# mLSTM query projection and scores: a float32 product against three float32r passes over high and low parts, last 128 columns float32, larger slot rings in list 5

## The chip, the core and the metric

The kernel runs on one core of a Trainium2 chip. A core has five engines that run side by side, each through its own queue in order: TensorE (PE, matrix products into PSUM, with its weight loads as PEld), VectorE (DVE), ScalarE (ACT), GpSimd (POOL) and SyncE (SP, which here issues most of the DMAs). An instruction waits at the head of its queue until the results that it needs are there, and everything behind it waits too. The metric is the device time of one execution in microseconds.

## What is computed

One inference step of a two-layer decoder trunk (native sparse attention, then mLSTM) for a prompt of 512 tokens and 8 sample tokens. All of the reference runs in the kernel; the change touches the mLSTM layer of the prompt, whose part of the reference is, cut down:

```python
D_MODEL, D_INNER, M_HEADS, M_HEAD_DIM, QKV_BLK = 1024, 2048, 4, 512, 4
c = jax.nn.silu(conv)
cb = c.reshape(B, T, nb, QKV_BLK)
q = jnp.einsum('btnj,nji->btni', cb, w_qkv[0]).reshape(B, T, D_INNER)
k = jnp.einsum('btnj,nji->btni', cb, w_qkv[1]).reshape(B, T, D_INNER)
...
S = jnp.einsum('bhtd,bhsd->bhts', qc, kc) * jnp.exp(D - mt[..., None])
num = jnp.einsum('bhts,bhse->bhte', S, vc) + ...
C = carry_decay[..., None, None] * C + jnp.einsum('bhsd,bhs,bhse->bhde', kc, w, vc)
```

The projections of q and k are block diagonal with blocks of 4. The kernel folds them: with `c` (the tile `CT`) as it stands, the scores of a head are `CT.T @ (M.T @ CT)`, where `M` is a block-diagonal 128x128 matrix (`bdm`) that holds the product of the q and k weights.

## The kernel before

All tensors are laid out with features on the 128 partitions and the 512 prompt tokens along the free dimension. The mLSTM width of 2048 is 16 tiles of 128 features, four for each of the four heads; a tile is named by head and place (`hd`, `kt`).

The kernel is written as lists of entries. A function such as `qk` adds entries with `P.op(engine, ..., function)`, and each function issues a few instructions. `P.run(ORDER2, R, NE, MOVEDP2)` then issues the entries of the fifth and longest planned stage, here called list 5, in the order that the tuple `ORDER2` gives. So `ORDER2` is the order of every engine's queue. An entry whose place is in `MOVEDP2` is moved to another engine: a copy on ScalarE goes to VectorE and the other way round, a subtraction, product or sum on VectorE goes to GpSimd and the other way round (`swapped`, line 642). `SLOTS` gives by hand which slot of a ring each tile of a pool takes; a tile that takes a used slot waits for that slot's last readers. The ring `("cella", "row")` has 9 slots of 128x512, `("cella", "bd")` 7 of 128x128.

List 5 holds 933 entries: 191 for TensorE, 282 for VectorE, 225 for ScalarE, 97 for GpSimd and 138 for SyncE once the moves are made. They are:

- `qk` (line 2558), for each of the 16 tiles: `f_bdm` and `f_bdk` build block-diagonal matrices; `f_ctw` weights the tile with a row from DRAM (`wb`); `f_po` is the projection `bdm.T @ CT`, one float32 matmul of 512 columns into PSUM; `f_q` copies it to SBUF; `f_s` adds this tile's part of the head's scores, four float32 matmuls of 512, 384, 256 and 128 columns (the scores are causal) into three PSUM banks; `f_pk`, `f_kwh`, `f_kwl`, `f_c`, `f_cpt` compute the state matrix `C` of the tile (for 13 of the 16 tiles; the other three come after list 5).
- `values` (line 2659), for each head: `f_w`, `f_a`, `f_m` turn the scores into weights, `f_h` and `f_l` split them (`Sh`, `Sl`), `f_n` multiplies them with the split values, `f_sq`, the additions to `acc`, `f_pd`, `f_pq`, `f_x1` to `f_y2` make the norm, `f_u1`, `f_u2`, `f_uh`, `f_ul` the gated and split output.
- `v_split`: the split of the values (`vh`, `vl`).
- `state_step` (line 2233), for 24 of the 32 states of the samples: a load of 2 x 512 KB (`cs`), `run` and `spread` on TensorE, `scale` on ScalarE, `outer` on VectorE, two stores.
- `out_unit` (line 2852): the output projection of the heads before, 12 float32r matmuls of 260 columns for each half (`prod`), with a split of the weights (`whi`, `wlo`) and an addition to `x`.
- `head_open` and `head_close`: small work on the samples; among it the copy into `QZ` that `run` reads.

A product that is not left in float32 is computed in three float32r passes over a high and a low part of each operand, high x high, high x low and low x high. The high part is a copy to float32r, the low part the difference:

```python
def lo_of(out, src, hi, eng=None):
    (eng or V).tensor_sub(out, src, hi.bitcast(F32))

def mm3(out, whi, wlo, xhi, xlo, start, stop):
    PE.matmul(out, whi, xhi, start=start, stop=False)
    PE.matmul(out, whi, xlo, start=False, stop=False)
    PE.matmul(out, wlo, xhi, start=False, stop=stop)
```

After list 5 comes the last list (line 2975): the output projection of head 3, the final norm, the three late tiles of `C`, and the last stores. It needs the split output `uh`, `ul` of head 3 from list 5.

Of the kernel before, what the change touches and what calls it, by code (L numbers as in the profile page):

```python
# [9 lines left out]
F32 = mybir.dt.float32  # L10
F32R = mybir.dt.float32r
# [400 lines left out]
    ("mi", "bd"): (
        0, 1, 2, 3, 0, 0, 1, 3, 0, 3, 2, 3, 1, 2, 1, 0,
    ),
    ("st0", "cse"): (
        0, 1, 2, 2, 1, 0, 1, 2, 0, 1, 2, 0, 1, 2, 0, 1, 0, 2, 1, 2, 0, 2, 1, 0, 1, 0, 2, 0,
    ),
# [2669 lines left out]
```

## Time and profile before

| | us |
|---|---|
| median of 3 runs (lowest to highest) | 995.83 (995.11 to 1001.67) |
| the profiled execution | 999.03 |
| its span, first to last instruction | 996.5 |
| granted clock of TensorE | 1.000 |
| bytes moved by DMA | 197.20 MB |

All instructions have the line number of one helper (L668), since the lists are recorded first and issued later, so groups are told apart by the tiles that they write and read: `mm<-CT,bdm` is `f_po`, `s<-q,CT` is `f_s`, `q<-mm` is `f_q`. A float32 matmul stands in the trace as two records, a float32r pass as one. A record's duration holds the pipeline's latency, so what a matmul costs in a full queue is the distance from its start to the next start. A row of a timeline has the start, the duration, the engine, the operation, `out<-in`, the shapes and a count; the idle time before it and what ended it stand in brackets. A row of grouped instructions has the busy time and the mean of one in ns, then the idle time before them.

### The profile page before, as it was taken

What the parts mean: (1) busy time and instruction counts of PE and PEld (TensorE: products, weight loads), DVE (VectorE), ACT (ScalarE), POOL (GpSimd) and SP (SyncE); (2) the same over time, 40 slices, a digit from 0 to 9 for tenths busy, and PEclk for the clock granted to TensorE, in tenths of its full rate; (3) what the DMA queues carried; (4) which work ended last, traced back from release to release, by engine and by line L of the source; (5) the groups of instructions that cost most, each with busy time, mean ns of one, the idle gap of its engine ahead of it and who ended that gap; (6) DMA issues with size and microseconds to landing.
All of it is one profiled execution on the core that took longest, in us unless ns stands there. A gap on an engine that the chain in (4) does not pass through costs nothing.

```text
span 996.5 us, 22671 instructions
## 1 busy us (share of the span) xinstructions
PE 973.9 (98%) x8329; PEld 860.4 (86%) x8329; DVE 797.8 (80%) x1922; ACT 556.0 (56%) x1224; POOL 336.3 (34%) x404
## 2 busy tenths in 40 slices
PE   7999998999999999999999999999999999999998
PEld 5799998899998878799999997998676768777897
DVE  7988986686499988856777997866787978699986
ACT  6746442423488788633346665547657464854533
POOL 1123434331233345622134224323332345424340
PEclk9999999999999999999999999999999999999999
DMA  8755631333445435644743465987997898987633
GB/s 290 244 165 187 202 117 65 112 112 128 149 123 155 127 109 156 184 155 178 213 159 124 137 215 172 319 283 254 286 313 282 293 323 255 326 281 268 210 128 117
DMA packets 123681, 197.20 MB, mean 198 GB/s; under 512 B 16165, under 2 KB 64550, under 8 KB 123314
## 3 DMA queue, kind: packets, MB, share of 16 engines
q1 hardware_dynamic: 117954, 185.39, 57.1%
q10 hardware_dynamic: 5616, 10.36, 2.8%
q8 instruction: 65, 1.06, 0.4%
q14 instruction: 46, 0.38, 0.1%
HBM read 145.99 MB, written 58.10 MB: 205 GB/s over the span
## 4 chain that ended last, share of the span: by engine, by line
PE 86%; DVE 8%; ACT 2%; DMA 2%; issue 1%; SPq 1%; POOL 0%; ACTq 0%; DVEq 0%; POOLq 0%
PE mm L668 55%; PE s L668 14%; PE t L668 12%; PE d L668 6%; DMA x_t<-in_xT 1%; DVE plo L668 1%; SPq L668 1%; DVE num L668 1%; DVE cs L668 1%; DMA praw<-in_cache 1%; DVE wlo L668 1%; DVE dn L668 0%; DVE x L668 0%; DVE ul L668 0%; ACT zsg L668 0%
## 5 line engine op out<-in xcount | busy, mean ns | idle before, releaser
L668 PE MATMUL mm<-hhi,whi 128*128 128x260 f32 x928 | 266.5, 287 | 0.2 <-DVE whi L668 0.2
L668 PE MATMUL mm<-hhi,wlo 128*128 128x260 f32 x928 | 262.4, 283 | 1.4 <-DVE wlo L668 1.4
L668 PE MATMUL mm<-hlo,whi 128*128 128x260 f32 x928 | 262.0, 282 | 0.0
L668 PEld LDWEIGHTS mm<-hhi,whi 128*128 128x128 f32 x928 | 174.7, 188 | 3.2 <-ACT zsg L668 0.8
L668 PEld LDWEIGHTS mm<-hhi,wlo 128*128 128x128 f32 x928 | 174.7, 188 | 1.9 <-DVE wlo L668 1.8
L668 PEld LDWEIGHTS mm<-hlo,whi 128*128 128x128 f32 x928 | 174.7, 188 | 1.1 <-issue 0.5
L668 POOL TENSOR_TENSOR wlo<-wraw,whi 128x512 fp32r<-128x512 f32 (+1 forms) x34 | 63.2, 1861 | 150.4 <-ACT whi L668 47.2
L668 DVE SCALAR_TENSOR_TENSOR cs<-t,wk,cs 128x512 f32<-128x512 f32 x128 | 88.5, 743 | 16.7 <-ACT cs L668 14.6
L668 DVE TENSOR_TENSOR wlo<-wraw,whi 128x1024 fp32r<-128x1024 f32 (+1 forms) x65 | 74.4, 1145 | 10.7 <-ACT whi L668 6.9
L668 ACT ACTIVATE whi<-wraw 128x1024 fp32r<-128x1024 f32 (+1 forms) x60 | 51.8, 868 | 54.7 <-PE mm L668 31.6
L668 ACT ACTIVATE cs<-cs,SBC 128x1024 f32<-128x1024 f32 x64 | 71.2, 1140 | 9.4 <-PE d L668 9.4
L668 ACT ACTIVATE s<-s,mn 128x256 f32<-128x256 f32 (+3 forms) x128 | 70.5, 555 | 7.6 <-DVE mn L668 4.9
L668 POOL TENSOR_SCALAR s<-s,sm 128x256 f32<-128x256 f32 (+3 forms) x53 | 50.6, 965 | 53.5 <-DVE sm L668 26.8
L668 PE MATMUL mm<-uh,whi 128*128 128x260 f32 x224 | 64.9, 290 | 0.7 <-DVE cs L668 0.7
L668 PE MATMUL mm<-uh,wlo 128*128 128x260 f32 x224 | 63.6, 284 | 1.0 <-POOL wlo L668 1.0
L668 PE MATMUL mm<-ul,whi 128*128 128x260 f32 x224 | 63.2, 282 | 0.0
L668 DVE CUSTOM_DVE_ANT_0 s<-s,D 128x128 f32<-128x128 f32 (+3 forms) x128 | 58.3, 486 | 5.5 <-PE s L668 4.0
L668 PE MATMUL s<-phi,w1a 128*128 128x256 f32 (+1 forms) x224 | 49.1, 297 | 0.0
L668 DVE TENSOR_TENSOR plo<-praw,phi 128x256 fp32r<-128x256 f32 (+1 forms) x50 | 41.3, 836 | 7.6 <-ACT phi L668 3.4
L668 PE MATMUL mm<-uo,whi 128*128 128x260 f32 x256 | 46.2, 283 | 0.0
L668 PEld LDWEIGHTS mm<-uh,whi 128*128 128x128 f32 x224 | 42.1, 188 | 2.4 <-DVE cs L668 0.8
L668 PEld LDWEIGHTS mm<-uh,wlo 128*128 128x128 f32 x224 | 42.1, 188 | 1.7 <-POOL wlo L668 1.4
(506 smaller groups left out, 2569.6 us busy)
## 6 DMA issues: line engine op xcount, KB each, us to landing
cs<-in_state_C SPq DMA_DIRECT2D x64, 512.0 KB, 5.6
o_cs<-cs SPq DMA_DIRECT2D x64, 512.0 KB, 4.4
praw<-in_cache SPq DMA_DIRECT2D x128, 128.0 KB, 3.3
dk<-in_cache SPq DMA_DIRECT2D x128, 128.0 KB, 2.6
wraw<-in_m_in SPq DMA_DIRECT2D x32, 512.0 KB, 4.0
wraw<-in_m_out SPq DMA_DIRECT2D x32, 256.0 KB, 4.7
wraw<-in_w_kv SPq DMA_DIRECT2D x11, 512.0 KB, 5.1
wraw<-in_w_q SPq DMA_DIRECT2D x8, 512.0 KB, 3.3
```

Source lines behind the costliest of these rows:

```text
L668: return f(*[real(x) for x in a], **{n: real(x) for n, x in k.items()})
```

## The change

In `qk`, both float32 products of a tile become float32r passes over split operands:

- the matrix `bdm` is split into `bh` and `bl` (128x128), the tile `CT` into `ch` and `cl` (128x512); `f_po` becomes three passes of 512 columns;
- the projection is read from PSUM three times: `f_qh` copies it to float32r, `f_ql` takes the difference (both 128x512), `f_qf` copies its last 128 columns in float32;
- `f_s` becomes three passes each for the blocks of 512, 384 and 256 columns, and the last block of 128 columns stays one float32 matmul with `qf`.

The rings grow: `row` from 9 slots to 15, `bd` from 7 to 13. Six more entries for each of 16 tiles make 1029 entries; `ORDER2`, `MOVEDP2` and the slot lists of list 5 are new throughout. After the moves there are 191 entries on TensorE, 328 on VectorE, 261 on ScalarE, 111 on GpSimd and 138 on SyncE. List 5's own work is otherwise the same, and nothing outside it is edited.

```diff
+    ROWB, BDB = 15, 13
...
-        bdk, bdm, ctw, q, kwh, kwl, cpt = (Tile_(n) for n in ("bdk", "bdm", "ctw", "q", "kwh", "kwl", "cpt"))
+        bdk, bdm, ctw, kwh, kwl, cpt = (Tile_(n) for n in ("bdk", "bdm", "ctw", "kwh", "kwl", "cpt"))
+        bh, bl, ch, cl, qf, qh, ql = (Tile_(n) for n in ("bh", "bl", "ch", "cl", "qf", "qh", "ql"))
...
+        def f_bh():
+            X["bh"] = c2.tile([128, 128], F32R, name="bh", tag="bd", bufs=BDB)
+            S.activation(X["bh"], X["bdm"], AF.Copy)
+
+        def f_bl():
+            X["bl"] = c2.tile([128, 128], F32R, name="bl", tag="bd", bufs=BDB)
+            lo_of(X["bl"], X["bdm"], X["bh"])
+
+        def f_ch():
+            X["ch"] = c2.tile([128, T], F32R, name="ch", tag="row", bufs=ROWB)
+            S.activation(X["ch"], ct, AF.Copy)
+
+        def f_cl():
+            X["cl"] = c2.tile([128, T], F32R, name="cl", tag="row", bufs=ROWB)
+            lo_of(X["cl"], ct, X["ch"])
...
         def f_po():
             X["po"] = mmb()
-            PE.matmul(X["po"], X["bdm"], ct, start=True, stop=True)
-
-        def f_q():
-            X["q"] = c2.tile([128, T], F32, name="q", tag="row", bufs=9)
-            S.activation(X["q"], X["po"], AF.Copy)
+            mm3(X["po"], X["bh"], X["bl"], X["ch"], X["cl"], True, True)
+
+        def f_qf():
+            X["qf"] = c2.tile([128, 128], F32, name="qf", tag="bd", bufs=BDB)
+            S.activation(X["qf"], X["po"][:, 384:512], AF.Copy)
+
+        def f_qh():
+            X["qh"] = c2.tile([128, T], F32R, name="qh", tag="row", bufs=ROWB)
+            S.activation(X["qh"], X["po"], AF.Copy)
+
+        def f_ql():
+            X["ql"] = c2.tile([128, T], F32R, name="ql", tag="row", bufs=ROWB)
+            lo_of(X["ql"], X["po"], X["qh"])
...
-                PE.matmul(st_out(hd, j), ct[:, ks], X["q"][:, 128 * j:], start=kt == 0 and j < 3, stop=kt == 3,
-                          skip_group_check=True)
+                if j == 3:
+                    PE.matmul(st_out(hd, j), ct[:, ks], X["qf"], start=False, stop=kt == 3, skip_group_check=True)
+                    continue
+                for n, (a, b) in enumerate((("ch", "qh"), ("ch", "ql"), ("cl", "qh"))):
+                    PE.matmul(st_out(hd, j), X[a][:, ks], X[b][:, 128 * j:], start=kt == 0 and n == 0,
+                              stop=kt == 3 and n == 2, skip_group_check=True)
...
+        P.op("ACT", 0.2, due - 4, f_bh, r=[bdm], new=[bh])
+        P.op("DVE", 0.2, due - 3, f_bl, r=[bdm, bh], new=[bl], lock=True)
+        P.op("ACT", 0.6, due - 3, f_ch, r=[CTI[ft]], new=[ch])
+        P.op("DVE", 0.68, due - 2, f_cl, r=[CTI[ft], ch], new=[cl], lock=True)
+        P.op("PE", 0.95, due, f_po, r=[bh, bl, ch, cl], new=[po])
+        P.op("ACT", 0.2, due + 1, f_qf, r=[po], new=[qf])
+        P.op("ACT", 0.6, due + 1, f_qh, r=[po], new=[qh])
+        P.op("DVE", 0.68, due + 1.6, f_ql, r=[po, qh], new=[ql])
```

(The figures in `P.op` are notes of a planner that made the order; they are not read when the kernel is built.)

More of the change, by code (lines that the diff above doesn't have):

```diff
@@ L415 @@
     ("st0", "cse"): (
-        0, 1, 2, 2, 1, 0, 1, 2, 0, 1, 2, 0, 1, 2, 0, 1, 0, 2, 1, 2, 0, 2, 1, 0, 1, 0, 2, 0,
+        0, 1, 2, 2, 1, 0, 1, 2, 0, 1, 2, 0, 1, 0, 2, 1, 0, 2, 1, 2, 0, 2, 1, 0, 2, 1, 0, 2,
     ),
@@ L427 @@
     ("st", "cs"): (
-        0, 1, 2, 3, 0, 1, 2, 3, 2, 1, 0, 3, 0, 1, 2, 3, 1, 3, 0, 1, 2, 1, 0, 3, 0, 1, 2, 3, 0, 1, 2, 3, 0, 3, 1, 2,
+        0, 1, 2, 3, 0, 1, 2, 3, 2, 1, 0, 3, 1, 0, 2, 3, 0, 2, 3, 1, 0, 3, 1, 2, 0, 3, 2, 1, 0, 2, 3, 1, 2, 0, 3, 1,
     ),
@@ L435 @@
     ),
+    ("cella", "row"): (
[4 rows of a table added]
+    ),
     ("cella", "bd"): (
-        0, 1, 2, 3, 4, 5, 6, 0, 1, 3, 2, 4, 6, 3, 1, 2, 1, 5, 5, 5, 0, 4, 5, 6, 1, 2, 3, 5, 4, 0, 1, 6,
-    ),
-    ("cella", "row"): (
-        0, 1, 2, 3, 4, 5, 6, 7, 8, 3, 2, 1, 4, 7, 0, 3, 2, 1, 4, 5, 2, 3, 5, 4, 2, 3, 5, 4, 7, 3, 2, 4, 7, 1, 8, 3,
-        0, 1, 5, 2, 4, 5, 1, 7, 0, 3, 8, 1, 2, 7, 1, 4, 5, 0, 2, 4, 7, 3, 1, 5, 2, 6, 2, 4, 1, 7, 3, 4, 6, 5, 1, 3,
[3 rows of a table added]
+    ),
+    ("fw", "w"): (
+        0, 1, 2, 3, 4, 5, 1, 0, 2, 3, 4, 1, 0, 5, 2, 4, 3, 1, 0, 2, 5, 4, 3, 0, 1, 3, 2, 5, 1, 0, 4, 5, 1, 2, 3, 1,
+        0, 4, 5, 2, 1, 0, 3, 2, 5, 4, 0, 3, 1, 2, 4, 5, 3, 0, 1, 4, 2, 5, 0, 3, 1, 2, 5, 4, 0, 1, 3, 4, 5, 2, 0, 3,
+        1, 2, 4, 5, 3, 0,
     ),
     ("cellb", "row"): (
-        0, 1, 2, 3, 4, 5, 2, 0, 1, 3, 4, 1, 0, 2, 5, 0, 3, 2, 1, 4, 5, 3, 2, 1, 0, 5, 4, 3, 2, 1, 4, 3, 1, 5, 0, 3,
-        1, 2, 4, 5,
-    ),
-    ("fw", "w"): (
-        0, 1, 2, 3, 4, 5, 1, 0, 3, 1, 5, 4, 2, 0, 1, 3, 2, 4, 5, 0, 3, 2, 1, 5, 0, 2, 3, 4, 2, 5, 0, 1, 4, 0, 3, 4,
-        0, 5, 2, 3, 1, 4, 3, 2, 0, 5, 4, 3, 0, 5, 1, 2, 3, 4, 0, 2, 4, 3, 0, 5, 1, 3, 2, 4, 0, 2, 4, 1, 5, 3, 0, 4,
-        2, 5, 3, 1, 0, 4,
+        0, 1, 2, 3, 4, 5, 3, 0, 2, 1, 5, 4, 0, 3, 2, 0, 4, 3, 1, 5, 3, 4, 1, 2, 3, 5, 0, 4, 1, 2, 0, 4, 1, 5, 3, 0,
+        4, 1, 2, 5,
     ),
@@ L2566, in rows @@
             def rows():
-                D["wb_", hd] = c2.tile([128, T], F32, name="wb", tag="row", bufs=9)
+                D["wb_", hd] = c2.tile([128, T], F32, name="wb", tag="row", bufs=ROWB)
                 SP.dma_start(D["wb_", hd], rd[hd, 1].unsqueeze(0).to_broadcast([128, T]))
@@ L2579, in f_bdk @@
         def f_bdk():
-            X["bdk"] = block_diag(c2, wc[:, 1, ft], "bdk", 7, "bd")
+            X["bdk"] = block_diag(c2, wc[:, 1, ft], "bdk", BDB, "bd")
         def f_bdm():
-            X["bdm"] = block_diag(c2, mw[:, ft], "bdm", 7, "bd")
+            X["bdm"] = block_diag(c2, mw[:, ft], "bdm", BDB, "bd")
+        def f_bh():
[10 more added lines that the diff above has]
+            lo_of(X["cl"], ct, X["ch"])
         def f_ctw():
-            X["ctw"] = big("ctw", n=T) if late else c2.tile([128, T], F32, name="ctw", tag="row", bufs=9)
+            X["ctw"] = big("ctw", n=T) if late else c2.tile([128, T], F32, name="ctw", tag="row", bufs=ROWB)
             V.tensor_tensor_reduce(X["ctw"], ct, D["wb_", hd], 1.0, 0.0, op0=OP.mult, op1=OP.add,
@@ L2604, in f_kwh @@
         def f_kwh():
-            X["kwh"] = c2.tile([128, T], F32R, name="kwh", tag="row", bufs=9)
+            X["kwh"] = c2.tile([128, T], F32R, name="kwh", tag="row", bufs=ROWB)
             S.activation(X["kwh"], X["pk"], AF.Copy)
         def f_kwl():
-            X["kwl"] = c2.tile([128, T], F32R, name="kwl", tag="row", bufs=9)
+            X["kwl"] = c2.tile([128, T], F32R, name="kwl", tag="row", bufs=ROWB)
             lo_of(X["kwl"], X["pk"], X["kwh"])
@@ L2626, in f_cpt @@
         def f_cpt():
-            X["cpt"] = c2.tile([128, T], F32, name="cpt", tag="row", bufs=9)
+            X["cpt"] = c2.tile([128, T], F32, name="cpt", tag="row", bufs=ROWB)
             S.activation(X["cpt"], X["pc"], AF.Copy)
@@ L2631, in qk @@
         P.op("DVE", 0.77, due - 1, f_ctw, r=[CTI[ft], D["wb", hd]], w=[("cwn", hd, kt)], new=[ctw], lock=True)
-        P.op("PE", 0.95, due, f_po, r=[bdm, CTI[ft]], new=[po])
-        P.op("ACT", 0.6, due + 1, f_q, r=[po], new=[q])
+        P.op("ACT", 0.2, due - 4, f_bh, r=[bdm], new=[bh])
[6 more added lines that the diff above has]
+        P.op("DVE", 0.68, due + 1.6, f_ql, r=[po, qh], new=[ql])
         if not late:
@@ L2638, in qk @@
         st = D["st", hd]
-        P.op("PE", 2.25, due + 2, f_s, r=[CTI[ft], q], w=["st%d" % hd] + ([] if kt == 0 else st), new=st if kt == 0 else [])
+        P.op("PE", 2.25, due + 2, f_s, r=[CTI[ft], qf, qh, ql, ch, cl], w=["st%d" % hd] + ([] if kt == 0 else st), new=st if kt == 0 else [])
         if not late:
@@ L2900, in step_kernel @@
             held += [D["pn", hd], D["wk", hd], D["pr", hd]]
-    P = Plan({**CAPS, "bdk": 5, "bdm": 2, "ctw": 2, "q": 2, "kwh": 1, "kwl": 1, "cpt": 2, "wb": 1, "zs": 1, "ab": 1, "wt": 2,
+    P = Plan({**CAPS, "bdk": 5, "bdm": 2, "ctw": 2, "qf": 2, "qh": 2, "ql": 2, "ch": 2, "cl": 2, "bh": 2, "bl": 2, "kwh": 1, "kwl": 1, "cpt": 2, "wb": 1, "zs": 1, "ab": 1, "wt": 2,
               "Sh": 1, "Sl": 1, "acc": 1, "sq1": 1, "hx": 1, "hy": 1, "fraw": FWB[0], "fhi": FWB[1], "flo": FWB[2]},
```

126 rows, old and new, of tables (MOVEDP2, ORDER2, SLOTS) are left out of this document.

## The prediction

> **What bounds the kernel now.** I read the page first (its busy shares and the chain that ended last), then a table of stretches over the part that list 5 orders, then the waits of VectorE, then single rows for prices.
>
> ```profile
> PE 973.9 (98%) x8329; PEld 860.4 (86%) x8329; DVE 797.8 (80%) x1922; ACT 556.0 (56%) x1224; POOL 336.3 (34%) x404
> PE 86%; DVE 8%; ACT 2%; DMA 2%; issue 1%; SPq 1%; POOL 0%; ACTq 0%; DVEq 0%; POOLq 0%
> ```
>
> ```profile
> core 0: us, PE busy (x) PEld busy (x) DVE busy (x) ACT busy (x) POOL busy (x), PEclk, DMA share, GB/s
> 711.00:740.00 29.00, 28.55 (x172) 17.60 (x173) 28.05 (x67) 17.88 (x26) 11.20 (x18) 1.00 0.89 292
> 740.00:813.00 73.00, 73.00 (x425) 52.82 (x424) 57.02 (x116) 43.16 (x72) 25.33 (x27) 1.00 0.87 300
> 813.00:880.00 67.00, 65.66 (x541) 53.70 (x541) 52.41 (x114) 38.77 (x66) 31.83 (x29) 1.00 0.89 292
> 880.00:960.00 80.00, 78.78 (x636) 66.97 (x635) 76.14 (x159) 38.30 (x69) 25.29 (x27) 1.00 0.75 251
> 711.00:960.00 249.00, 245.99 (x1768) 191.09 (x1769) 213.62 (x453) 138.11 (x232) 93.66 (x100) 1.00 0.84 281
> ```
>
> The first row pair says that TensorE carries the end (86% of the chain). The table says that this is not the whole story inside list 5, which runs from about 711 to 960 us. TensorE is busy in 246.0 of 249 us. VectorE is busy in 213.6 and idle in 35.4, and its idle time is spread unevenly: 16.0 us in 740 to 813, 14.6 in 813 to 880, but 1.0 in 711 to 740 and 3.9 in 880 to 960. In those last 80 us both engines are full. ScalarE (138) and GpSimd (94) have room everywhere, and the clock is 1.00 throughout.
>
> ```profile
> DVE cs L668 <- ACT cs L668: 9.9, 7, 4.3
> DVE hx L668 <- ACT hx L668: 4.1, 2, 3.3
> DVE x L668 <- PE mm L668: 3.5, 4, 1.6
> DVE dn L668 <- PE t L668: 3.1, 1, 3.1
> ```
>
> These are VectorE's longest waits (total, times, longest). They are waits in a fixed queue for results that TensorE or ScalarE gave late. They are slack as long as TensorE is the bound; the question is how much of it new VectorE work can fill.
>
> **TensorE: what the passes save.** Prices are start to start, since matmuls overlap.
>
> ```profile
> 728.35 2.77 PE mm L668 x12
> 765.24 0.89 PE t L668 x8
> 766.13 0.86 PE mm L668 x2
> 766.99 2.16 PE s L668 x8
> 919.08 0.39 PE L668 MATMUL mm<-Sh,vh 128*128 128x512 f32 x1
> ...
> 920.67 0.22 PE L668 MATMUL mm<-Sh,vh 128*128 128x128 f32 x1
> ...
> 920.95 0.45 PE L668 MATMUL mm<-Sh,vh 128*128 128x512 f32 x1
> ```
>
> Here 766.13 is one `f_po` (a float32 product of 512 columns, two records): 0.86 us. 766.99 is one `f_s` (512, 384, 256 and 128 columns in float32, eight records): 2.16. 728.35 is one `f_c`, twelve float32r passes of 512 columns: 2.77, or 0.23 each. So the new `f_po` costs 3 x 0.23 = 0.69, a gain of 0.17. From 919.08 to 920.67 run nine float32r passes, three each of 512, 384 and 256 columns, exactly what the new `f_s` issues: 1.59. Its last block stays a float32 product of 128 columns; 765.24 holds four of those in 0.89, so 0.22. (Three passes of 128 took 920.67 to 920.95, 0.28, so leaving that block in float32 is right.) New `f_s`: 1.81, a gain of 0.35. Sixteen tiles: 16 x (0.17 + 0.35) = **8.3 us less TensorE work**. This price is firm: the same shapes and types stand in the trace.
>
> **VectorE: what the splits cost.** I set the new list 5 and its moved entries against the code, entry by entry. The 16 of each new kind run: `f_bl` 5 on VectorE and 11 on GpSimd; `f_cl` 7 and 9; `f_ql` all 16 on VectorE; `f_bh` 10 on VectorE and 6 on ScalarE; `f_ch` 4 and 12; `f_qf` 5 and 11; `f_qh` 2 and 14. The old `f_q` had 5 on VectorE and 11 on ScalarE.
>
> ```profile
> 947.41 1.89 DVE L668 TENSOR_TENSOR num<-num,zs 128x512 f32<-128x512 f32 x3
> 715.15 0.42 DVE L668 CAST vh<-VT 128x512 fp32r<-128x512 f32 x1
> L668 DVE TENSOR_TENSOR bdm<-cst,mw 128x128 f32<-128x128 f32 x6 | 1.7, 280 | 0.0
> L668 DVE COPY q<-mm 128x512 f32<-128x512 f32 x5 | 3.4, 683 | 0.0
> L668 DVE SCALAR_TENSOR_TENSOR wt<-s,wt 128x128 f32<-128x128 f32 x4 | 1.1, 280 | 0.0
> ```
>
> Three 128x512 operations take 1.89 with 0.08 of overlap each: 0.60 a piece. Less the same overlap a 128x512 cast is 0.34, a PSUM copy of 128x512 0.60, a 128x128 operation 0.20. The trace has no 128x128 cast on VectorE; it lies between nothing and the 0.20 above, and I take 0.14. Sum: `f_bl` 1.0, `f_cl` 4.2, `f_ql` 9.6, `f_bh` 1.4, `f_ch` 1.4, `f_qf` 1.0, `f_qh` 1.2, less 3.0 for `f_q`: 16.8 us. The other entries that change engine (five more additions to `acc`, four more `ul` and two more `Sl` come to VectorE, three `vl`, a copy of `ncs`, a `cpt` and some casts go) come to about 2. So **19 us more VectorE work**.
>
> ```profile
> L668 DVE TENSOR_TENSOR kwl<-t,kwh 128x512 fp32r<-128x512 f32 x13 | 8.9, 686 | 2.9 <-ACT kwh L668 2.7
> L668 DVE TENSOR_TENSOR ul<-num,uh 128x512 fp32r<-128x512 f32 x8 | 6.5, 839 | 1.1 <-POOL ul L668 1.1
> 910.01 1.77 DVE L668 TENSOR_TENSOR Sl<-wt,Sh 128x512 fp32r<-128x512 f32 x1
> ```
>
> VectorE is also stretched now and then: a subtraction with one PSUM input (`kwl`) takes 686 ns on the mean, the same shape with both inputs in SBUF (`ul`) 839, one `Sl` 1.77 us. The excess is 0.15 for `ul`; about 14 more such operations on VectorE and more GpSimd work beside them make about 2 us. Total: 21, so VectorE busy goes from 213.6 to **234.6 us**. [...]
>
> **The other engines.**
>
> ```profile
> L668 ACT ACTIVATE vh<-VT 128x512 fp32r<-128x512 f32 x10 | 6.2, 619 | 0.7 <-issue 0.7
> L668 ACT ACTIVATE q<-mm 128x512 f32<-128x512 f32 x11 | 6.5, 589 | 3.8 <-PE mm L668 3.8
> L668 ACT ACTIVATE onesr<-ones 128x128 fp32r<-128x128 f32 x1 | 0.3, 299 | 0.0
> L668 POOL TENSOR_TENSOR vl<-VT,vh 128x512 fp32r<-128x512 f32 x8 | 10.7, 1333 | 13.3 <-DVE vl L668 11.3 <-ACT vh L668 1.8
> L668 POOL TENSOR_TENSOR bdm<-cst,mw 128x128 f32<-128x128 f32 x10 | 4.0, 404 | 8.6 <-PE t L668 8.6
> ```
>
> ScalarE gains 12 `f_ch` at 0.62, 6 `f_bh` and 11 `f_qf` at 0.30 and three more copies at 0.59: 14 us, hidden in its 111 idle us. GpSimd gains 11 x 0.40 + 9 x 1.33 = 16 and gives about 8 away: hidden too. SyncE keeps its 138 entries and all bytes; loads stand in another order, DMA is 0.84 busy over the stretch, and the same bytes in 246 us make 0.85. I price that and the larger rings of slots (row 9 to 15, bd 7 to 13, which issue nothing) at nothing; a load or a slot that comes late would show as a VectorE or ScalarE wait, so the ends are those of the idle time below.
>
> The chain for one tile grows: the product now waits for `f_ch` and `f_cl`, and the scores wait for `f_qh` and then `f_ql`. Behind a late `f_ql` stand VectorE's `outer` entries, which stores wait for, and behind a late `f_s` all of TensorE. The tightest place in the new list is tile 3 of head 2, where between `f_po` and `f_s` TensorE has one `f_s` and one `spread` (over 2.0 us), against 0.6 + 0.6 plus hand-over for the chain. It fits. The opening doesn't:
>
> ```profile
> 711.45 1.12 PE mm L668 x2
> 712.58 2.21 PE d L668 x16
> ```
>
> Before, two `f_po` run ahead of or during the wait for `QZ`; now the first `f_po` stands behind the 16 products of 712.58 and needs a cast, two subtractions and `f_bdm` of VectorE after it has written `QZ`. I take 1.5 us lost there (between 0 and the 2.5 that both products and one subtraction take).
>
> **The sum.** If TensorE stayed the bound the part would shorten by 8.3 to 240.7, and VectorE, busy 234.6, could idle in only 6. I don't believe it. Where both engines are full in this trace (880 to 960) VectorE still idles 3.9 of 80, or 4.8%. At that rate 234.6 becomes 246.4: **a gain of 2.6 us**.
>
> A second count agrees. The last stage begins with
>
> ```profile
> 876.58 0.86 PE t L668 x2
> 877.56 0.68 DVE L668 SCALAR_TENSOR_TENSOR hx<-t,hx 128x512 f32<-128x512 f32 x1
> 957.79 1.42 DVE L668 TENSOR_TENSOR x<-x,mm 128x260 f32<-128x260 f32 x4
> ```
>
> which are `f_pq` and `f_x4` of head 2 and the end of list 5 on VectorE: 82 us, VectorE full. Behind that `f_x4` stood 100 VectorE entries and now stand 104, nine of them new (4 us) for others that went. So this stage doesn't shorten. Ahead of that `f_pq` TensorE saves 12 tiles' worth, 6.2 us, but has 133 entries instead of 130 (about 3 us at 1 us each) and loses 1.5 at the opening: 2 us left. What TensorE saves in head 3 is late for nobody: VectorE is late next. I take **2.3 us less**. The profiled execution took 999.03 (2.5 around its span of 996.5), so such a one would take 996.7; the median of the runs is 995.83, 3.2 lower, so I say **993.5**.
>
> **The rivals.** *VectorE keeps its idle time* (the other side). For it: its waits above are for ScalarE's `cs` and `hx`, not for TensorE alone, and a fixed queue with two more hand-overs per tile fills badly. Against: the first and the last stage fill it. Price: with 25 of 35.4 us kept, 234.6 + 25 = 259.6, 10.6 more than 249, so 1006.4. It turns into a loss where more than 14.4 us of idle stay.
>
> *TensorE stays the bound.* For it: 246 of 249 busy, new entries placed early (34 of the 49 new VectorE entries stand ahead of `f_x4` of head 1, where 17 us were idle). Against: the 6 us that it leaves VectorE. Price: 8.3 less, 987.5; with the 3 us that TensorE now idles saved as well, 984.5.
>
> *GpSimd and VectorE block each other in full.* For it: 910.01. Against: the mean excess is 0.15 of 1.3. If each of the net 8 us of new GpSimd work held VectorE up, VectorE would be 8 us later: 246.4 + 8 - 2 (counted already) = 252.4, 3.4 slower, 999.2. [...]
>
> **Chances.** My forecast, with TensorE and VectorE both near full and -6 to +3 us: 0.58. TensorE stays the bound: 0.17. Blocking in full: 0.10. VectorE keeps its idle time: 0.15. A measurement of this kernel can tell about 1% (10 us) from no change. Faster by more than that needs the second rival with its stalls gone: 0.10. Slower by more than that needs most of the first: 0.13. The rest, 0.77, is within 1%. The range of 985 to 1004 runs from the TensorE bound with part of its stalls gone to 22 us of VectorE idle (+7.6, 1003.4).
>
> **What would show it.** In the after profile `f_po` should take 0.7 and `f_s` 1.8 start to start, and TensorE's busy time from 711 to the end of list 5 should be under 240. VectorE's busy time there should be near 234 with 8 to 16 idle. If VectorE's idle is over 20, with TensorE waits on `ql` or `cl`, the first rival holds; if TensorE is full and VectorE waits for it, the second; if `wlo`, `ul` and `cl` rows of VectorE exceed 1 us often, the third. A price of a float32r pass far from 0.23 would make the whole sum wrong.

## The result and the profile after

| | before | after |
|---|---|---|
| median of 20 runs each, side by side on one chip (lowest to highest) | 997.66 (995.11 to 1002.52) | 990.37 (987.80 to 996.94) |
| the profiled execution | 999.03 | 989.0 |
| its span | 996.5 | 987.3 |

The changed kernel takes 0.9933 of the time before, with a 95% interval of 0.9918 to 0.9949: 6.7 us less (5.1 to 8.2). The median of 995.83 us, from which the prediction started, was that of the first three runs; over twenty it is 997.66.

All instructions now have line L677. The page's busy shares and the chain that ended last, of the kernel after:

```profile
PE 966.8 (98%) x8393; PEld 868.4 (88%) x8393; DVE 810.3 (82%) x1968; ACT 568.2 (58%) x1260; POOL 342.3 (35%) x418
PE 7%; DVE 4%; issue 1%; ACT 1%; POOL 0%; DVEq 0%; ACTq 0%; POOLq 0%
```

TensorE has 64 more records and is busy 7.1 us less. The chain could be followed back over the last eighth of this execution only, so its shares can't be set against the 86% of before. Its pieces can be read (start, duration, what):

```profile
875.67 0.68 DVE hx L677
...
888.56 1.81 PE s L677 x11
...
922.06 1.41 DVE cs L677 x2
...
946.75 1.79 DVE ul L677 x3
```

A new `f_s` takes 1.81 us, as worked out. From 922 to 949 us the chain goes no longer through TensorE but, bar a few pieces, through VectorE: the norm of head 3 and what stands in its queue. (875.67 is `f_x4` of head 2.)

The same table of stretches as before, cut at 953 us, just behind the new end of list 5 (950.3):

```profile
core 0: us, PE busy (x) PEld busy (x) DVE busy (x) ACT busy (x) POOL busy (x), PEclk, DMA share, GB/s
711.00:740.00 29.00, 29.00 (x199) 22.77 (x193) 25.09 (x63) 23.11 (x41) 15.01 (x24) 0.98 0.90 301
740.00:813.00 73.00, 72.96 (x493) 59.74 (x492) 68.17 (x144) 50.85 (x92) 35.18 (x40) 1.00 0.90 307
813.00:880.00 67.00, 64.51 (x535) 54.04 (x534) 63.39 (x125) 35.49 (x60) 23.91 (x24) 1.00 0.89 298
880.00:953.00 73.00, 72.56 (x615) 63.79 (x614) 70.07 (x162) 39.37 (x72) 27.08 (x29) 1.00 0.74 247
711.00:953.00 242.00, 239.03 (x1835) 200.34 (x1829) 226.72 (x490) 148.81 (x265) 101.18 (x116) 1.00 0.85 286
```

VectorE is busy in 226.7 of 242 us, where it was busy in 213.6 of 249. In the two middle stretches (740 to 880) its idle time has gone from 30.6 us to 8.4. TensorE is still full (239.0 of 242 us). VectorE's waits:

```profile
DVE cs L677 <- ACT cs L677: 5.7, 6, 2.2
DVE ql L677 <- ACT qh L677: 1.7, 2, 1.3
```

The waits for `hx`, `mm` and `dn` of before are gone or short; 5.7 us for ScalarE's `cs` remain, and 1.7 us for the new `qh`.

Prices of the new VectorE work, first by groups, then two rows of the opening, and the end of list 5 on VectorE:

```profile
L677 DVE TENSOR_TENSOR ql<-mm,qh 128x512 fp32r<-128x512 f32 x16 | 10.9, 685 | 1.9 <-ACT qh L677 1.7
L677 DVE TENSOR_TENSOR cl<-CT,ch 128x512 fp32r<-128x512 f32 x7 | 6.4, 922 | 0.0
```

```profile
708.66 0.23 DVE L677 CAST bh<-bdm 128x128 fp32r<-128x128 f32 x1
708.80 1.29 DVE L677 TENSOR_TENSOR cl<-CT,ch 128x512 fp32r<-128x512 f32 x2
...
946.66 1.97 DVE L677 TENSOR_TENSOR ul<-HN,uh 128x8 fp32r<-128x8 f32 x4
948.55 1.75 DVE L677 TENSOR_TENSOR x<-x,mm 128x260 f32<-128x260 f32 x5
```

`f_ql` takes what a subtraction with a PSUM input took before (`kwl`, 686 ns). Two `f_cl` take 1.29 us where nothing is beside them, 0.65 each, but 922 ns on the mean: two of the seven last longer, 1.23 us at 778.37 and 1.81 at 868.50, the one beside GpSimd's `Sl` (778.21, 0.84 us) and `bl` (779.02, 0.91), the other beside its `vl` (868.47, 1.29).

TensorE's own waits in list 5:

```profile
PE d L677 <- DVE QZ L677: 2.0, 1, 2.0
PE mm L677 <- DVE kwl L677: 1.8, 1, 1.8
...
PE mm L677 <- DVE ql L677: 0.2, 1, 0.2
```

The two long waits stand at single places; for a new split (`ql`) it waits 0.2 us in all.

Not all of the 9.2 us between the two spans belongs to the change. The row `t<-pr,ones`, the same piece of work just ahead of list 5 in both kernels, starts at 708.06 us before and 705.10 after (both rows are shown below). So 3.0 us had been gained where the two kernels are the same, and 6.2 us from there on, which agrees with the runs.

### The profile page after: what moved, and what is told of

Read it like the earlier page. It is cut to its first block, busy times and chain, and to the rows that moved or that the text cites. A ratio compares the mean times of both kernels' runs of the same rounds, so it can differ in the third digit from the quotient of the medians.

```text
span 987.3 us, 22906 instructions
## 1 busy us (share of the span) xinstructions
PE 966.8 (98%) x8393; PEld 868.4 (88%) x8393; DVE 810.3 (82%) x1968; ACT 568.2 (58%) x1260; POOL 342.3 (35%) x418
## 5 line engine op out<-in xcount | busy, mean ns | idle before, releaser
L677 PE MATMUL mm<-hhi,whi 128*128 128x260 f32 x928 | 266.4, 287 | 0.2 <-DVE whi L677 0.2
L677 PE MATMUL mm<-hhi,wlo 128*128 128x260 f32 x928 | 262.4, 283 | 1.4 <-DVE wlo L677 1.3
L677 PE MATMUL mm<-hlo,whi 128*128 128x260 f32 x928 | 262.0, 282 | 0.0
L677 PEld LDWEIGHTS mm<-hhi,whi 128*128 128x128 f32 x928 | 174.7, 188 | 3.2 <-PE d L677 0.8
L677 PEld LDWEIGHTS mm<-hhi,wlo 128*128 128x128 f32 x928 | 174.8, 188 | 2.1 <-DVE wlo L677 2.0
L677 PEld LDWEIGHTS mm<-hlo,whi 128*128 128x128 f32 x928 | 174.7, 188 | 1.1 <-issue 0.5
L677 POOL TENSOR_TENSOR wlo<-wraw,whi 128x512 fp32r<-128x512 f32 (+1 forms) x35 | 64.4, 1842 | 121.9 <-DVE whi L677 43.1
L677 DVE SCALAR_TENSOR_TENSOR cs<-t,wk,cs 128x512 f32<-128x512 f32 x128 | 88.7, 742 | 11.2 <-ACT cs L677 10.4
L677 DVE TENSOR_TENSOR wlo<-wraw,whi 128x1024 fp32r<-128x1024 f32 (+1 forms) x64 | 73.9, 1155 | 10.4 <-ACT whi L677 6.5
L677 ACT ACTIVATE cs<-cs,SBC 128x1024 f32<-128x1024 f32 x64 | 71.3, 1146 | 12.5 <-PE d L677 10.4
L677 ACT ACTIVATE s<-s,mn 128x256 f32<-128x256 f32 (+3 forms) x128 | 70.6, 555 | 7.6 <-DVE mn L677 4.9
L677 ACT ACTIVATE whi<-wraw 128x1024 fp32r<-128x1024 f32 (+1 forms) x59 | 51.2, 871 | 41.1 <-PE mm L677 26.7
L677 POOL TENSOR_SCALAR s<-s,sm 128x256 f32<-128x256 f32 (+3 forms) x53 | 50.6, 965 | 53.9 <-DVE sm L677 27.1
L677 PE MATMUL mm<-uh,whi 128*128 128x260 f32 x224 | 65.0, 290 | 1.8 <-DVE kwl L677 1.8
L677 PE MATMUL mm<-uh,wlo 128*128 128x260 f32 x224 | 63.6, 284 | 0.3 <-POOL wlo L677 0.3
L677 PE MATMUL mm<-ul,whi 128*128 128x260 f32 x224 | 63.3, 283 | 0.3 <-DVE ul L677 0.3
L677 DVE CUSTOM_DVE_ANT_0 s<-s,D 128x128 f32<-128x128 f32 (+3 forms) x128 | 58.3, 485 | 5.5 <-PE s L677 4.1
L677 PE MATMUL s<-phi,w1a 128*128 128x256 f32 (+1 forms) x224 | 49.1, 297 | 0.0
L677 PE MATMUL mm<-uo,whi 128*128 128x260 f32 x256 | 46.2, 283 | 0.0
L677 PEld LDWEIGHTS mm<-uh,whi 128*128 128x128 f32 x224 | 42.1, 188 | 3.8 <-DVE kwl L677 2.0
L677 DVE TENSOR_TENSOR plo<-praw,phi 128x256 fp32r<-128x256 f32 (+1 forms) x50 | 39.1, 792 | 7.1 <-ACT phi L677 4.0
L677 PEld LDWEIGHTS mm<-ul,whi 128*128 128x128 f32 x224 | 42.2, 188 | 1.3 <-issue 0.5
```

What stands on the lines that cost most here:

```text
L677: return f(*[real(x) for x in a], **{n: real(x) for n, x in k.items()})
```

## The experiments

Each row is a ratio to runs of the kernel before on the same chip. The last column is the difference of its ratio to 0.9933, times 997 us; two such intervals together leave 2.0 to 2.5 us of doubt in it, and more in two runs with few executions: 3.1 in early_unlocked, 3.8 in no_ql_two_passes. Where a length of list 5 is given, it is that of one profiled execution.

| run | median | ratio, 95% interval | against the changed kernel |
|---|---|---|---|
| float32_again | 998.22 | 1.0011 (0.9995 to 1.0028) | +7.8 |
| old_work_new_order | 996.48 | 0.9991 (0.9976 to 1.0006) | +5.8 |
| no_ql | 990.01 | 0.9924 (0.9911 to 0.9937) | -0.9 |
| two_passes | 988.09 | 0.9915 (0.9898 to 0.9933) | -1.8 |
| no_ql_two_passes | 985.33 | 0.9886 (0.9852 to 0.9921) | -4.7 |
| splits_on_vector | 998.25 | 1.0017 (0.9999 to 1.0035) | +8.4 |
| splits_heads01 | 994.58 | 0.9969 (0.9949 to 0.9989) | +3.6 |
| splits_heads23 | 994.50 | 0.9966 (0.9948 to 0.9984) | +3.3 |
| before_unlocked | 997.36 | 0.9999 (0.9984 to 1.0014) | (edit of the kernel before) |
| early_po | 990.02 | 0.9932 (0.9912 to 0.9951) | -0.1 |
| unlocked_alone | 988.27 | 0.9922 (0.9904 to 0.9939) | -1.1 |
| early_unlocked | 987.81 | 0.9897 (0.9871 to 0.9924) | -3.6 |

**float32_again: the products alone undone.** The theory was that TensorE set the time and its saving is the gain; the rival, that the gain came with the new order, the moves and the rings.

```diff
-            mm3(X["po"], X["bh"], X["bl"], X["ch"], X["cl"], True, True)
+            PE.matmul(X["po"], X["bl"].bitcast(F32), X["cl"].bitcast(F32), start=True, stop=True)
...
-                for n, (a, b) in enumerate((("ch", "qh"), ("ch", "ql"), ("cl", "qh"))):
-                    PE.matmul(st_out(hd, j), X[a][:, ks], X[b][:, 128 * j:], start=kt == 0 and n == 0,
-                              stop=kt == 3 and n == 2, skip_group_check=True)
+                PE.matmul(st_out(hd, j), X["cl"].bitcast(F32)[:, ks], X["ql"].bitcast(F32)[:, 128 * j:], start=kt == 0,
+                          stop=kt == 3, skip_group_check=True)
```

> The changed kernel with one float32 matmul again for each projection and for each block of the scores (on the low parts alone, so the products of the high parts are left out); every split and every wait of the change stays. TensorE gets its 8.3 us back, VectorE's work is the same. If TensorE still sets the time of list 5: 6 to 8 us above the changed kernel's 990.4, so 996 to 999. If VectorE sets it, or if the gain is the new order's alone: 0 to 2 above, 990 to 993.

998.22 us, 7.8 us more: all of the gain hangs on the 8.3 us of TensorE work. The profile shows where it falls. These are `f_x4` of head 2 and the end of list 5 on VectorE:

```profile
881.44 0.69 DVE L677 SCALAR_TENSOR_TENSOR hx<-t,hx 128x512 f32<-128x512 f32 x1
956.30 1.75 DVE L677 TENSOR_TENSOR x<-x,mm 128x260 f32<-128x260 f32 x5
```

From the row `t<-pr,ones` to this `f_x4`, and from there to the end, list 5 takes:

| us | to `f_x4` of head 2 | from there to the end |
|---|---|---|
| before | 169.5 | 81.7 |
| float32_again | 176.0 | 76.6 |
| the changed kernel | 170.6 | 74.6 |

The new list, with its splits, shortens the last part by 5.0 us and lengthens the part ahead by 6.5. The passes then take 5.4 and 2.0 us off the two parts, near the 6.2 and 2.1 at which the twelve tiles ahead and the four behind were priced.

**old_work_new_order: the order alone.** The old products and the old copy, without the splits (`f_bh` stays, as a float32 copy), in the new order, with the new moves and rings.

```diff
-            mm3(X["po"], X["bh"], X["bl"], X["ch"], X["cl"], True, True)
+            PE.matmul(X["po"], X["bh"], ct, start=True, stop=True)
...
-            lo_of(X["cl"], ct, X["ch"])
+            R.flip = None
...
-            lo_of(X["ql"], X["po"], X["qh"])
+            R.flip = None
```

> The new order, new moves and larger rings with the old float32 products: no low parts, no f_ch, no f_qf; only f_bh stays, as a float32 copy of the matrix. VectorE has about 15 us less work than in the changed kernel, TensorE 8.3 more. If the gain is the order's (and its fewer collisions): 985 to 991. If TensorE's saving is needed: 996 to 999. If both engines share the bound: in between, 991 to 995.

996.48 us, a ratio of 0.9991 to before: the order, the moves and the rings bring nothing by themselves. The other half, the new work in an order like the old one, wasn't tried, so what the order and the larger rings are worth to the new work stays open.

**no_ql: VectorE lighter.**

```diff
-            lo_of(X["ql"], X["po"], X["qh"])
+            R.flip = None
...
-                for n, (a, b) in enumerate((("ch", "qh"), ("ch", "ql"), ("cl", "qh"))):
+                for n, (a, b) in enumerate((("ch", "qh"), ("ch", "qh"), ("cl", "qh"))):
```

> The changed kernel without the 16 low parts of the projection (f_ql); the second pass of the scores reads the high part once more, so the low part's share is left out and TensorE does the same work. VectorE has 16 x 0.60 = 9.6 us less and the chain from projection to scores is shorter. If VectorE sets the time: 5 to 9 us below 990.4, 981 to 985. If TensorE sets it: 0 to 2 below, 988 to 990.

990.01 us. Taking 9.6 us of work from VectorE brings nothing that can be measured (in the profile its busy time over list 5 falls by 7.0 us, from 228.6 to 221.6). With the first run this makes TensorE the bound of the changed kernel as far as `f_ql` reaches. The last one starts at 896.9 us, so of the end of list 5, where the chain runs through VectorE from 922 us on, the run says nothing.

**two_passes: TensorE lighter.**

```diff
-                for n, (a, b) in enumerate((("ch", "qh"), ("ch", "ql"), ("cl", "qh"))):
+                for n, (a, b) in enumerate((("ch", "qh"), ("ch", "ql"))):
...
-                              stop=kt == 3 and n == 2, skip_group_check=True)
+                              stop=kt == 3 and n == 1, skip_group_check=True)
```

> The changed kernel without the third pass (low part of the tile times high part of the projection) in the scores, which is left out of the sum; all splits stay. TensorE has 16 x 0.53 = 8.4 us less, VectorE the same. If TensorE sets the time: 6 to 8 us below 990.4, 982 to 985. If VectorE sets it: 0 to 2 below, 988 to 990. Both engines at their limit: 2 to 4 below.

988.09 us: of another 8.4 us of TensorE work only about 2 come through (list 5 is 3.6 us shorter, 241.7 against 245.2). TensorE now waits 1.9 us in all for `ql`, where it waited 0.2. Another limit stands right behind TensorE, and the remaining runs ask which one.

**no_ql_two_passes: both lighter.** The two diffs above together.

> From the changed kernel, two cuts together: the 16 f_ql are left out (the second score pass reads qh in place of ql; VectorE -9.6 us) and the third score pass is left out (TensorE -8.4 us). Alone the first gave 990.0 and the second 988.1, against 990.4 for the changed kernel. Theory VECTORE IS NEXT: TensorE sets the time of the changed kernel, and with 8.4 us less of it VectorE, busy 226.7 of 242 us, stops the gain after 2.3 us. With VectorE lighter too, most of the 8.4 us arrive: 982 to 985. Rival SOMETHING ELSE IS NEXT (waits of the fixed order, the opening, loads, the last list): 987 to 988.5, no better than the cut in TensorE alone.

985.33 us. The cut in VectorE, worth 0.9 alone, is worth 2.9 once TensorE is lighter, and TensorE's 1.9 us of waits for `ql` go with it. That points to VectorE as the next limit, but does not show it: the doubt in 2.9 is 3.9 us, and list 5 is only 0.8 us shorter than in two_passes (240.9 against 241.7). Nor is 4.7 the whole 8.4: the first theory's range was just missed, and the rival's too. What keeps the other 3.7 us is not settled. Part of it is TensorE's granted clock at the opening (more on that below): 0.63 and 0.52 in the two stretches of 4 us from 708 in this profile, 0.59 and 0.98 in the changed kernel's, which makes an estimate of 1.7 us.

**splits_on_vector, and its two halves: VectorE heavier.** The places of the 20 `f_cl` and `f_bl` leave the list of moved entries, so GpSimd's share of the splits goes back to VectorE.

```diff
-MOVEDP2: 313, 331, 349, 351, 459, 475, 477, 493, 495 (heads 0 and 1)
-MOVEDP2: 583, 585, 601, 619, 621, 637, 794, 814, 824, 826, 838 (heads 2 and 3)
```

> From the changed kernel, the 9 f_cl and 11 f_bl that run on GpSimd go back to VectorE: VectorE +7.6 us of work by the prices of the prediction, GpSimd -16. Theory VECTORE HAS ROOM (it idles 15 us in list 5): 990 to 992.5. Rival VECTORE IS AT ITS LIMIT: most of 7.6 us comes through, 995 to 998. Third possibility: VectorE is freed of blocks by those 20 GpSimd instructions and gets that much back, so that its busy time rises by less than 7.6.

998.25 us: 8.4 more for 7.6 us of work, so nearly all of it comes through, although VectorE idled 15 us. In the profile VectorE is busy 235.0 us in list 5, against 228.6, so 6.4 of the 7.6 us arrive there; a little is given back, as the third possibility had it. TensorE's waits show how the work comes through:

```profile
PE mm L672 <- DVE cl L672: 2.5, 1, 2.5
PE s L672 <- DVE ql L672: 2.3, 2, 2.1
```

Both are new, bar the 0.2 us for `ql`, and with them list 5 is 4.7 us longer (249.9 against 245.2). This execution, 993.81 us, was the shortest of its twelve. Over the twelve the mean granted clock of TensorE is 0.9948, over the changed kernel's twenty 0.9970; on TensorE's 967 us that makes an estimate of 2 of the 8.4 us. Is it the sum of the work or these two places? Each half was run by itself.

> From the changed kernel, of the 20 f_cl and f_bl that run on GpSimd only the 9 of heads 0 and 1 go back to VectorE (VectorE +3.4 us of work). All 20 together took 998.2 against 990.4. Theory THE AMOUNT: VectorE as a whole is at its limit, so each part brings its own work: 993.5 to 994.5. Rival THE PLACE: the chain of a tile is late where its splits wait their turn in VectorE's queue, and TensorE stands (in the profile of all 20 it waited 2.1 us for a ql of head 1 near 757 us and 2.5 us for a cl): this half brings most of the 7.8 us, 995 to 998, with these TensorE waits in it.

> From the changed kernel, the other 11 of the 20 (heads 2 and 3: 5 f_cl, 6 f_bl; VectorE +4.2 us of work) go back to VectorE. Theory THE AMOUNT: 994 to 995. Rival THE PLACE: 990 to 992, since no TensorE wait of the profile of all 20 stood here but the 2.5 us for a cl.

994.58 and 994.50 us: 3.6 and 3.3 more for 3.4 and 4.2 us of work, about where THE AMOUNT had put them. But each half has kept one of the two waits, heads 0 and 1 first:

```profile
PE s L672 <- DVE ql L672: 2.1, 1, 2.1
```

```profile
PE mm L672 <- DVE cl L672: 2.5, 1, 2.5
```

In the second half's profile list 5 is 3.1 us longer (248.3 us), which is this wait and one of 0.6 us for a `cs`. In the first half's it is 5.0 us longer (250.2): the wait of 2.1, and a lower clock behind it and at the opening (0.994 over this whole execution, against 0.998 in the changed kernel's), each an estimate of 1.7 us from the granted clock of its stretches. So two places, each with its own wait, could give the same medians. The runs don't tell the amount from the places, and the profiles speak for the places.

**before_unlocked: was VectorE the bound of the last stage before?** In the kernel before, six GpSimd entries of the last stage (three `wlo`, three of the gated output of head 2), beside which VectorE's rows stood stretched (from 899 to 927 us rows of 1.59, 1.77, 1.71, 1.22 and 1.30 us, where the shortest of their kinds take 0.68, 0.68, 0.68, 0.19 and 0.17), go to VectorE (one that was moved there leaves the list, one that is written for GpSimd joins it).

```diff
-MOVEDP2: 700, 889
+MOVEDP2: 702, 704, 790, 875
```

> From the kernel before, six GpSimd entries of the last stage (three wlo, three of the gated output of head 2), each of which overlaps a stretched VectorE instruction, are moved to VectorE: VectorE +3.6 us of work, and about 8.7 us of stretch less in that stage. Theory of the prediction (VECTORE SETS THE LAST STAGE of the kernel before): 3 to 5 us faster than before, 992 to 994. Rival TENSORE SETS IT TOO: within 1 us of before, 996.5 to 998, with VectorE's busy time in 880 to 960 lower and its idle time higher.

997.36 us, no change. Some of VectorE's rows in the kernel before, and the same in this one:

```profile
914.22 1.71 DVE L668 TENSOR_TENSOR ul<-num,uh 128x512 fp32r<-128x512 f32 x1
...
917.17 1.22 DVE L668 TENSOR_TENSOR HN<-HN,CS 128x32 f32<-128x32 f32 x1
```

```profile
916.12 0.69 DVE L664 TENSOR_TENSOR ul<-num,uh 128x512 fp32r<-128x512 f32 x1
...
919.16 0.19 DVE L664 TENSOR_TENSOR HN<-HN,CS 128x32 f32<-128x32 f32 x1
```

What took 1.71 and 1.22 us takes 0.69 and 0.19. The stretch of 880 to 960 us in its profile:

```profile
880.00:960.00 80.00, 77.35 (x617) 64.81 (x616) 73.25 (x159) 39.93 (x71) 17.55 (x23) 1.00 0.75 249
```

VectorE's busy time in it is 73.25 us, where it was 76.14. But this execution is the longest of its twelve (1002.21 us) and starts list 5 later (710.40 us against 708.06), so the stretch is not the same work. From `f_x4` of head 2 to the end of the list, in each kernel's own time, VectorE is busy 76.5 of 83.2 us, and was 77.0 of 81.7. It has 2 us more of idle time, and the stage is no shorter. So VectorE did not set the pace of the last stage, and part of its fullness there was stretch, as in the 1.71 and 1.22 us above. That leaves TensorE, busy in 80.4 of those 81.7 us; in the new list float32_again agrees, where 2.1 us less TensorE work there made that part 2.0 us shorter.

**early_po: the opening.** Tiles 0 and 1 of head 0 get one float32 product again, ahead of the first `run`, with `f_bdm` on GpSimd; their `f_bh` and `f_bl` fall away.

```diff
+    EARLY = ((0, 0), (0, 1))
...
         def f_po():
             X["po"] = mmb()
+            if (hd, kt) in EARLY:
+                PE.matmul(X["po"], X["bdm"], ct, start=True, stop=True)
+                return
             mm3(X["po"], X["bh"], X["bl"], X["ch"], X["cl"], True, True)
```

> From the changed kernel, the first two projections (tiles 0 and 1 of head 0) are single float32 products again, as before the change, and stand ahead of the first run; their two f_bdm are on GpSimd, their f_bh and f_bl fall away. TensorE pays 2 x 0.17 = 0.34 us more, VectorE is 0.9 us lighter. Theory THE OPENING COSTS 2 US: TensorE waits 2.03 us for QZ there and the two products (1.7 us) fill the hole, so the scores of tile 0 start 1 to 1.7 us sooner and the time is 988.5 to 989.5. Rival THE HOLE IS HARMLESS: TensorE starts the scores sooner, but the time comes back as a wait further on: 990.0 to 991.0.

990.02 us: nothing that can be measured, with 2.5 us of doubt. The timeline of TensorE at the opening, first of the kernel before, then of the changed one, then of early_po:

```profile
708.06 0.27 PE L668 MATMUL t<-pr,ones 128*32 128x32 f32 x8 [1.33 <-DVE pr L668]
709.71 1.12 PE L668 MATMUL mm<-CT,bdm 128*128 128x512 f32 x2 [0.36 <-POOL bdm L668]
711.45 1.12 PE L668 MATMUL mm<-CT,bdm 128*128 128x512 f32 x2 [0.62 <-DVE bdm L668]
712.51 2.28 PE L668 MATMUL d<-cs,QZ 128*32 128x512 f32 x16
```

```profile
705.10 0.27 PE L677 MATMUL t<-pr,ones 128*32 128x32 f32 x8 [1.33 <-DVE pr L677]
...
708.42 3.53 PE L677 MATMUL d<-cs,QZ 128*32 128x512 f32 x16 [2.03 <-DVE QZ L677]
...
712.79 0.40 PE L677 MATMUL mm<-ch,bh 128*128 128x512 f32 x1
...
713.49 0.62 PE L677 MATMUL t<-VB,OH 128*128 128x512 f32 x2
```

```profile
706.61 0.27 PE L608 MATMUL t<-pr,ones 128*32 128x32 f32 x8 [1.34 <-DVE pr L608]
...
708.25 1.98 PE L608 MATMUL mm<-CT,bdm 128*128 128x512 f32 x4 [0.35 <-POOL bdm L608]
710.17 1.92 PE L608 MATMUL d<-cs,QZ 128*32 128x512 f32 x16
...
714.52 0.39 PE L608 MATMUL s<-qh,ch 128*128 128x512 f32 x1
```

The hole of 2.03 us is filled, and the first scores come 7.9 us after `t<-pr,ones` instead of 9.5 (714.64 in the changed kernel). In the traces list 5 is 1.1 us shorter (from that row to the last `ul`: 242.4 against 243.5 us); in the runs it doesn't show.

**unlocked_alone and early_unlocked: stretched rows in the changed kernel.** Six GpSimd entries of 840 to 872 us (three `f_u2` and an `f_ul` of head 1, two `vl`) go to VectorE, alone and together with the edit before.

```diff
-MOVEDP2: 565, 784, 786
+MOVEDP2: 555, 563, 567
```

> From the changed kernel, two edits together: the first two projections as float32 products ahead of the first run (as in the run early_po), and six GpSimd entries of 840 to 872 us (three products and a subtraction of the gated output of head 1, two vl) on VectorE, where VectorE instructions stood blocked beside them for 6.7 us in sum (one of them, 1.06 us in the norm of the samples, ahead of TensorE's wait of 1.8 us for kwl); VectorE +3.6 us of work. Theory BLOCKS COST HERE: TensorE's 1.8 us wait goes and the opening's 1.1 us that the trace of early_po showed stays saved: 987.5 to 989. Rival VECTORE IS AT ITS LIMIT: the 3.6 us of work undo it: 990 to 993.

> From the changed kernel, only the second edit of early_unlocked: the six GpSimd entries of 840 to 872 us on VectorE, the opening as it is. Both together took 987.8, the opening alone 990.0, the changed kernel 990.4. Theory BLOCKS BRING IT: 988 to 989, with TensorE's wait of 1.8 us for kwl gone and its wait of 2.0 us for QZ still there. Rival BOTH ARE NEEDED: as long as the opening's wait and lowered clock stay, 989.5 to 990.5.

987.81 us for both edits, 3.6 less than the changed kernel (with 3.1 us of doubt) and 0.9897 of the kernel before (0.9871 to 0.9924): the fastest of all kernels here that leave nothing out. The second edit alone has 988.27 us, but by its ratio only 1.1 less, within the doubt. The traces are clearer (VectorE, the changed kernel, then unlocked_alone):

```profile
846.02 1.23 DVE L677 SCALAR_TENSOR_TENSOR hf_v<-rs_t,rs_y 128x8 f32<-128x8 f32 x1
847.28 1.19 DVE L677 TENSOR_TENSOR dn<-hf_v,dn 128x8 f32<-128x8 f32 x1
...
848.62 0.68 DVE L677 TENSOR_TENSOR kwl<-t,kwh 128x512 fp32r<-128x512 f32 x1
```

```profile
846.70 0.17 DVE L672 SCALAR_TENSOR_TENSOR hf_v<-rs_t,rs_y 128x8 f32<-128x8 f32 x1
846.90 0.17 DVE L672 TENSOR_TENSOR dn<-hf_v,dn 128x8 f32<-128x8 f32 x1
...
847.21 0.68 DVE L672 TENSOR_TENSOR kwl<-t,kwh 128x512 fp32r<-128x512 f32 x1
```

And GpSimd and TensorE of the changed kernel at the same time:

```profile
845.92 2.53 POOL L677 TENSOR_TENSOR num<-num,zs 128x512 f32<-128x512 f32 x2
```

```profile
849.36 0.39 PE L677 MATMUL mm<-uh,whi 128*128 128x260 f32 x1 [1.78 <-DVE kwl L677]
```

Two operations on 128x8 that take 0.17 us each took 1.23 and 1.19 beside two GpSimd products; `kwl` behind them came late, and TensorE stood for 1.78 us. In unlocked_alone this wait is gone, and list 5 is 2.7 us shorter (240.8 against 243.5, to the last `ul`). VectorE's busy time over list 5 falls too, from 228.6 to 226.2 us, though it got 3.6 us of work. With the opening's edit added the list is no shorter still (241.0).

## Where the prediction was right and where it failed

The forecast was 993.5 us, within 985 to 1004, with both engines near full; 990.37 came, and both engines are near full. The gain was mis-sized: 2.3 us were forecast and 6.7 came (5.1 to 8.2), just past the 6 that bounded my own case, and nearer to the 8.3 of the rival in which TensorE stays the bound. That the time itself lies only 3.1 us from the forecast is in part luck: the three runs from which I started had a median of 995.83 us and twenty have 997.66, and the errors of the steps below partly cancel. By its steps:

- **TensorE saves 8.3 us: right.** A new `f_po` takes 0.70 us (712.79 to 713.49), a new `f_s` 1.81; 16 x (0.16 + 0.35) = 8.2. Putting the old products back costs 7.8.
- **TensorE as the only bound, 8.3 us less: nearly reached.** 6.7 of the 8.3 us came. TensorE does set the time while VectorE gets lighter (no_ql), but it waits 1.8 us for a late `kwl`, and 2.0 at the opening.
- **Both engines near full: right, and closer than thought.** 8.3 us more TensorE work cost 7.8, and 7.6 us more VectorE work 8.4; 8.4 us less on TensorE brought about 2, and 9.6 less on VectorE about 1, each with some 2 us of doubt. So another limit, most likely VectorE's queue, lies some 2 us behind TensorE's.
- **VectorE's work, 19 us more: right as far as the rows go.** `f_ql` takes 685 ns on the mean, like the `q` copy (683) that priced it, and a 128x128 cast 0.14 us (708.66 to the next start at 708.80), the value taken between nothing and 0.20. Over the whole of list 5 VectorE's busy time rose by 14.1 us, from 214.5 to 228.6; with about 4 us less of stretch (next step) that is some 18 us of work.
- **Two us more stretch: wrong, in sign.** By this step VectorE was to be busy 234.6 us; it is busy 226.7. Summed over list 5, what VectorE's instructions take beyond the shortest of their kind is about 21 us before and 17 after (19 and 16 if the shortest is taken within each kernel). The new moves put other GpSimd work beside VectorE, above all in the last stage, where eleven instructions stretched by 0.15 to 1.12 us became two (0.50 and 1.10).
- **The length from VectorE's busy time and 4.8% of idle time: wrong as a rule.** VectorE idles 15.3 us of 242, or 6.3%, within the 8 to 16 us named as a sign. But with the measured 226.7 us the sum gives 238.1, a gain of 10.9 us. Its two terms erred in opposite directions. VectorE's busy time did not set the length: 9.6 us less of its work brought nothing that could be measured.
- **The second count, last stage the same and 2 us less ahead of it: wrong in both parts.** The last stage went from 81.7 us to 74.6 (877.56 to 959.21 before, 875.67 to 950.30 after), and the part ahead grew from 169.5 to 170.6. The row of VectorE's busy time, 3.9 us idle of 80, was read as a bound; before_unlocked shows that it wasn't. Of the 7.1 us, 5.0 came with the new list and 2.0 with the passes (float32_again), so what TensorE saves in head 3 was not late for nobody. That this count agreed with the first was chance.
- **The opening loses 1.5 us: the right place, its effect open.** TensorE waits 2.03 us there for `QZ`, and then runs its 16 products in 3.53 us instead of 2.28. Filling the hole gave 1.1 us in the trace and nothing measurable in the runs.
- **ScalarE, GpSimd, loads and rings at nothing: right** as far as the order alone shows it (0.9991); but room on GpSimd is worth something: the 20 splits that it carries cost 8.4 us when VectorE has to do them.

Of the rivals, GpSimd and VectorE blocking each other in full was wrong as a forecast, and right at single places: at 846 us two 128x8 operations, from 846.02 to 848.47, last as long as the two GpSimd products beside them, from 845.92 to 848.45. The first, idle time kept, fell: 20 of 35 us went.

## What to carry to other kernels

Busy time is not work: ahead of calling an engine full, take out of its busy time what its instructions last beyond the shortest of their form (here about 21 of 214.5 us before), and see what runs beside them. A full row of busy time is not a bound until a run with less of that work is shorter. Where two engines are near full, cutting one brought little here (0.9 us for 9.6 on VectorE, 1.8 for 8.4 on TensorE) and loading either cost about in full (8.4 us for 7.6 and 7.8 for 8.3), so a trade between them pays only until they meet. Look for small operations that run beside a GpSimd instruction and stand ahead of something that TensorE waits for: here two of 0.17 us took 1.23 and 1.19, and TensorE stood for 1.78 us. Moving the GpSimd work away removed that wait, though it gave VectorE 3.6 us more work.

## What the runs showed that was not expected

The granted clock of TensorE fell at the opening, in the changed kernel but not in the one before. Stretches of 4 us, the changed kernel first, then before, then early_po (the clock is the first of the three figures at the end):

```profile
704.00:708.00 4.00, 1.29 (x16) 0.89 (x16) 2.60 (x16) 2.57 (x9) 0.35 (x2) 1.00 0.93 252
708.00:712.00 4.00, 3.58 (x17) 1.05 (x17) 3.90 (x16) 3.17 (x7) 0.51 (x2) 0.59 1.02 298
```

```profile
704.00:708.00 4.00, 2.73 (x23) 2.52 (x22) 1.90 (x8) 2.19 (x7) 0.93 (x2) 1.00 0.90 299
708.00:712.00 4.00, 2.96 (x20) 1.49 (x20) 2.70 (x16) 2.19 (x8) 1.08 (x3) 1.00 0.95 308
```

```profile
704.00:708.00 4.00, 2.56 (x27) 1.95 (x25) 1.95 (x11) 2.18 (x6) 1.12 (x3) 1.00 0.86 257
708.00:712.00 4.00, 3.75 (x20) 1.09 (x20) 2.88 (x13) 3.71 (x11) 0.56 (x2) 1.00 0.94 312
```

Where TensorE was busy in 1.29 of 4 us, its clock went to 0.59 in the next four, and the 16 products of the first `run`s took 3.53 us; where it was busy in 2.73 and 2.56 of 4, the clock stayed at 1.00 and they took 2.28 and 1.92. The difference, 1.3 to 1.6 us, is an estimate of what the wait of 2 us cost behind it. In all ten profiles with the changed kernel's opening the clock falls in 708 to 712 us (0.50 to 0.82; 0.57 in splits_on_vector, 0.61 in unlocked_alone), in seven of them below 0.9 in the next 4 us too, and in none of the four with the opening of before or of early_po (1.00 in before_unlocked too). Over the whole profiled execution the clock is 0.994 to 0.998 in the ten, and 1.000 in the four but for before_unlocked (0.998). In splits_heads01 it falls once more, to 0.84 and 0.74 in the 8 us from 756, around its wait of 2.1 us for `ql`. In the changed kernel's trace the fall at the opening comes after two gaps of 1.33 and 2.03 us with little work between them; the kernel before has gaps of 1.33, 0.36 and 0.62 us there, and its clock stayed at 1.00.
